# 203 groups of unread matmuls behind the last layer of a two-layer attention trunk

## The chip, the cores and the metric

The kernel runs on one core of one Trainium2 chip. The metric is the device time of one execution in microseconds. The profile is one execution with the hardware profiler on; its span goes from the first to the last instruction.

## The reference

The input x has 256 positions of 2048 channels. Two layers follow each other. A layer multiplies x with one wide matrix, cuts the result into queries, keys, values and gates of two attention branches with twelve heads each, does the attention of both, multiplies the gated results up to 2048 channels, mixes them with sigmoid gates, multiplies once more and normalises:

```python
h = jnp.einsum('bsd,dc->bsc', x, w_in)
...
out_a = dilated_mixture(qa, ka, heads(va, N_HEADS_A)).reshape(B, S, WIDTH_A)
up_a = jnp.einsum('bsw,wd->bsd', out_a * jax.nn.silu(za), w_up_a)
...
out_b = forgetting_attention(heads(qb, N_HEADS_B), heads(kb, N_HEADS_B),
                             heads(vb, N_HEADS_B), log_f).reshape(B, S, WIDTH_B)
up_b = jnp.einsum('bsw,wd->bsd', out_b * jax.nn.silu(zb), w_up_b)
...
y = jnp.einsum('bsd,de->bse', g_a * up_a + g_b * up_b, w_out)
return layer_norm(DEEPNORM_ALPHA * x + y, ln_g, ln_b)
```

The change adds nothing to what is computed.

## The kernel before

The state is kept transposed: channels in the partitions, the 256 positions (`S`) in the columns. So that the float32r matmuls keep their precision, every operand is held as two float32r numbers, a high part and a low part (`split`: ACT copies the high part, DVE subtracts). x lies in eight tiles `xs`, each for two blocks of 128 channels; `x_at(k)` is the block k with its high 256 columns followed by its low 256, 512 words in a row. There are sixteen such blocks (`KT`).

Weights come over the SP queue as pieces (`Piece`): mostly eight blocks of 128 x 128 for one output tile of 128 channels. A piece is split into a buffer `w` of 2240 words a partition, six of which are used in rotation. The high part begins at word 48 (`W_OFF`), the low part `W_PART` = 1088 words behind it. For the values the weights are 256 (once 268) columns wide and begin at word 16 (`V_OFF`).

A unit is one output tile of 128 channels. Its matmuls (`stat_mm`) keep the weights stationary and move x; they are pairs:

```python
            if part == 1:
                nc.tensor.matmul(o, w[:, 1], a[:, 0], start=False, stop=last)
            elif halves == 2:
                nc.tensor.matmul(ps(), w[:, 0], a, start=first, stop=False)
```

The high weights (line 161) move all 512 columns, the low weights (line 159) only the 256 high ones. Within a piece all `part` 0 go first and then all `part` 1, so runs of eight 512-column matmuls stand before runs of eight 256-column ones; the units over the gated heads have pieces of six blocks. Only in the three units that open a layer does each pair stand by itself, 512 and 256 columns in turn. The value units (`v_mm`, lines 345 to 352) are turned: x is stationary, the weights move (line 350: high and low weights of 256 columns each, line 352: high weights alone), for two output tiles in turn. The very last unit (lines 163, 164, 159) takes 256 columns at a time.

All these outputs are PSUM tiles `mm`, four in rotation, which ACT and DVE read out (lines 170 and 172; for the last projection 467 to 469). At the start, and between the layers, `keep_warm` adds matmuls of a zero tile whose result is not read (line 136).

Behind the last unit stands the normalisation: `second` sums over the channels by one-column matmuls (line 510), `ln_stats` forms mean and scale and spreads them over the partitions by matmuls again (line 523), and `ln_apply` normalises on DVE, ACT and GpSimd and stores the eight tiles over the SP queue (line 579).

The program is written unit by unit; a scheduler then orders each engine's instructions by their dependencies, so later work can be put between earlier work that waits. Each engine executes its own list in order.

Of the kernel before, what the change touches and what calls it, by code (L numbers as in the profile page):

```python
# [10 lines left out]
F32 = mybir.dt.float32  # L11
F32R = mybir.dt.float32r
# [6 lines left out]
S = 256  # L19
# [4 lines left out]
KT = D // 128  # L24
# [10 lines left out]
W_PART = (SLOT + 63) // 64 * 64  # L35
# [5 lines left out]
def trunk(ctx: ExitStack, tc: tile.TileContext, xt, w_st, w_v, w_vf, w_up, w_o,  # L41
          b_f, b_g, ln_g, ln_b, rope_c, bias_a, mask_c, ident_c, yt):
    nc = tc.nc
# [4 lines left out]
    wp = ctx.enter_context(tc.tile_pool(name="wp", bufs=1))  # L48
# [4 lines left out]
    pmm = ctx.enter_context(tc.tile_pool(name="pmm", bufs=4, space=PSUM))  # L53
# [554 lines left out]
    while n < len(units):  # L608
        k = 3 if n in interleaved else 1
# [55 lines left out]
    stats()  # L665
    for j2 in range(KT // 2):
        apply(j2)


def _tables():  # L670
# [78 lines left out]
```

## Time and profile before

| | us |
|---|---|
| median of two runs | 1984.47 (1984.30 to 1984.65) |
| profiled execution | 1984.45 |
| its span | 1982.7 |
| TensorE busy in the span | 1961.7 |
| VectorE (DVE) busy | 1269.7 |
| ScalarE (ACT) busy | 985.7 |
| GpSimd busy | 76.5 |
| mean granted TensorE clock | 0.994 |

The profiled execution is 1.75 us longer than its span: what lies ahead of the first and behind the last instruction. A busy engine is one with an instruction under way; matmuls overlap, so the number of matmuls times their mean duration is more than the busy time, and what one costs is read from the distance between two starts. In a timeline, a row merges instructions of one line that follow each other: its first number is the start of the first.

### The profile page before, as it was taken

The page shows a single profiled execution, that of the slowest core. Times are in us where ns is not written, and L with a number is a line of the kernel's source. Part 1 is how long each engine was busy: PE and PEld are TensorE (multiplying, and loading weights), DVE is VectorE, ACT ScalarE, POOL GpSimd, SP SyncE. Part 2 cuts the span into 40 slices and gives each one's busy share as a digit, 9 for nine tenths or more (in the row PEclk, how much of TensorE's full clock was granted, in tenths as well). Part 3 has the DMA queues.
Part 4 walks back from the last instruction along what each step waited for, and adds up shares of the span by engine and source line. Part 5 has one row for each costly group of instructions (what it writes and reads, how often), then busy time and mean ns, then how long its engine had stood idle before and what let it go on. Part 6 is the DMA issues. An engine that isn't in the chain of part 4 may idle for free.

```text
span 1982.7 us, 29718 instructions
## 1 busy us (share of the span) xinstructions
PE 1961.7 (99%) x11449; PEld 1730.0 (87%) x11449; DVE 1269.7 (64%) x1896; ACT 985.7 (50%) x1555; POOL 76.5 (4%) x69
## 2 busy tenths in 40 slices
PE   9999999999999999999999999999999999999997
PEld 7888888889888888888888888888898888888886
DVE  7666665556555556668777666655555555556686
ACT  5444444454444445554455444445454444545544
POOL 0000000001000000001200000000010000000022
PEclk9999999999999999999999999999999999999998
DMA  8655555666556655665555555566666655556651
GB/s 300 199 177 178 179 165 171 193 194 211 185 184 180 182 165 177 185 206 194 159 171 179 171 181 176 165 183 183 205 201 186 187 177 180 170 173 190 210 183 63
DMA packets 107766, 362.74 MB, mean 183 GB/s; under 512 B 12368, under 2 KB 15592, under 8 KB 107624
## 3 DMA queue, kind: packets, MB, share of 16 engines
q1 hardware_dynamic: 106600, 357.68, 58.2%
q0 software_dynamic: 1024, 3.17, 0.7%
q8 instruction: 89, 1.46, 0.3%
q14 instruction: 53, 0.43, 0.1%
HBM read 358.68 MB, written 2.12 MB: 182 GB/s over the span
## 4 chain that ended last, share of the span: by engine, by line
PE 98%; DVE 1%; ACT 0%; DMA 0%; issue 0%
PE mm L161 53%; PE mm L159 27%; PE mm L350 8%; PE mm L352 4%; PE ps_s L255 1%; PE po L284 1%; PE pt L275 1%; PE po L285 1%; PE ps_s L254 1%; DMA raw<-xt 0%; PE mm L348 0%; PE mm L345 0%; PE mm L346 0%; ACT gated L573 0%; PE mm L163 0%; PE mm L164 0%
## 5 line engine op out<-in xcount | busy, mean ns | idle before, releaser
L68 DVE TENSOR_TENSOR w<-raw,w 128x1024 fp32r<-128x1024 f32 (+3 forms) x713 | 840.3, 1183 | 448.4 <-ACT w L67 447.1
L67 ACT ACTIVATE w<-raw 128x1024 fp32r<-128x1024 f32 (+3 forms) x713 | 716.7, 1008 | 457.3 <-issue 221.8
L161 PE MATMUL mm<-x,w 128*128 128x512 f32 x3328 | 855.9, 396 | 7.5 <-DVE x L560 4.8
L161 PEld LDWEIGHTS mm<-x,w 128*128 128x128 f32 x3328 | 599.1, 188 | 116.9 <-issue 5.1
L159 PEld LDWEIGHTS mm<-x,w 128*128 128x128 f32 x3328 | 453.9, 188 | 34.2 <-DVE w L68 0.3
L159 PE MATMUL mm<-x,w 128*128 128x256 f32 x3328 | 469.6, 279 | 0.0
L170 ACT ACTIVATE c<-mm 128x256 f32<-128x256 f32 x320 | 120.4, 384 | 458.7 <-PE mm L159 425.0
L172 DVE TENSOR_TENSOR p<-mm,c 128x256 f32<-128x256 f32 x252 | 106.7, 424 | 185.9 <-ACT c L170 185.4
L161 PE MATMUL mm<-gated,w 128*128 128x512 f32 x768 | 196.5, 391 | 0.0
L350 PE MATMUL mm<-w,x 128*128 128x512 f32 x704 | 176.7, 393 | 0.0
L161 PEld LDWEIGHTS mm<-gated,w 128*128 128x128 f32 x768 | 135.2, 188 | 21.2
L350 PEld LDWEIGHTS mm<-w,x 128*128 128x128 f32 x704 | 126.1, 188 | 22.6
L161 PE MATMUL mm<-merged,w 128*128 128x512 f32 x480 | 120.1, 392 | 0.0
L159 PEld LDWEIGHTS mm<-gated,w 128*128 128x128 f32 x768 | 108.3, 188 | 10.4
L159 PE MATMUL mm<-gated,w 128*128 128x256 f32 x768 | 111.2, 279 | 0.0
L352 PEld LDWEIGHTS mm<-w,x 128*128 128x128 f32 x704 | 94.7, 188 | 7.4
L161 PEld LDWEIGHTS mm<-merged,w 128*128 128x128 f32 x480 | 85.9, 188 | 15.5 <-DVE merged L68 0.5
L352 PE MATMUL mm<-w,x 128*128 128x256 f32 x704 | 96.5, 279 | 0.0
L159 PEld LDWEIGHTS mm<-merged,w 128*128 128x128 f32 x512 | 68.2, 188 | 4.7
L159 PE MATMUL mm<-merged,w 128*128 128x256 f32 x512 | 70.1, 279 | 0.0
L444 POOL TENSOR_TENSOR u<-x 128x512 f32<-128x512 f32 x16 | 31.7, 1982 | 603.8 <-DVE merged L68 484.2
L264 ACT ACTIVATE z<-z,s 128x128 f32<-128x128 f32 x96 | 42.3, 444 | 0.0
(129 smaller groups left out, 918.0 us busy)
## 6 DMA issues: line engine op xcount, KB each, us to landing
raw<-w_st SPq DMA_DIRECT2D x410, 512.0 KB, 3.7
raw<-w_up SPq DMA_DIRECT2D x128, 384.0 KB, 3.2
raw<-w_v SPq DMA_DIRECT2D x88, 512.0 KB, 4.3
raw<-w_o SPq DMA_DIRECT2D x64, 512.0 KB, 3.7
raw<-w_vf SPq DMA_DIRECT2D x8, 536.0 KB, 3.7
nb<-cum POOLq DMA_DIRECT2D x12, 256.0 KB, 4.5
raw<-w_st SPq DMA_DIRECT2D x9, 256.0 KB, 5.6
yt<-gated SPq DMA_DIRECT2D x8, 256.0 KB, 2.1
```

Source lines behind the costliest of these rows:

```text
L67: nc.scalar.activation(hi, src, AF.Copy)
L68: nc.vector.tensor_tensor(lo, src, hi.bitcast(F32), op=ALU.subtract)
L159: nc.tensor.matmul(o, w[:, 1], a[:, 0], start=False, stop=last)
L161: nc.tensor.matmul(ps(), w[:, 0], a, start=first, stop=False)
L170: nc.scalar.activation(c, ps[:, S:], AF.Copy, scale=scale)
L172: nc.vector.tensor_tensor(dst, ps[:, :S], c, op=ALU.add)
L254: nc.tensor.matmul(ps[:, 0], q[:, :128], k[:, :128], start=True, stop=True)
L255: nc.tensor.matmul(ps[:, 1:3].rearrange("p a b -> p (a b)"), q[:, 128:], k, start=True, stop=True)
L264: nc.scalar.activation(z[:, sl], z[:, sl], AF.Exp, scale=-1.0, bias=s4[:, c:c + 1], accum_out=s4[:, 2 + c:3 + c])
L350: nc.tensor.matmul(o, xh, w, start=first, stop=False)
L352: nc.tensor.matmul(o[:, :NV], xl, w[:, 0], start=False, stop=last)
L444: nc.gpsimd.tensor_tensor(u, x[:, :, 0], x[:, :, 1], op=ALU.add)
```

## The change

A function `timing` is called behind the last layer. It takes two of the `w` buffers, fills them with zeros by two memsets on DVE, and issues matmuls of these weights with the x that the last layer was given. The results go into `mm` tiles and are not read.

`pairs(hi, lo, cut)` is one group of the first kind: sixteen pairs as in `stat_mm`, in runs of the lengths in `cut` (first the 512-column matmuls of the run, then its 256-column ones), the high weights beginning at word `hi` and the low ones at `W_PART + lo`. There are 3 groups of (8, 8), then for each run length of 1, 2, 4, 8 and 16 one group at each of the sixteen combinations of 0, 16, 32 and 48 for `hi` and `lo`, then eight uneven cuts three times each at four combinations. `turned(o, run)` is a group of the second kind, as in the value units, with two output tiles and the weights beginning at word `o`: three run lengths, four places, twice each. That makes 3 + 80 + 96 + 24 = 203 groups.

```diff
--- before.py
+++ after.py
@@ -665,6 +665,63 @@
     stats()
     for j2 in range(KT // 2):
         apply(j2)
+    timing(nc, wp, pmm, x_at)
+
+
+def timing(nc, wp, pmm, x_at):
+
+    ts = []
+    for _ in range(2):
+        t = wp.tile([128, 2 * W_PART + 64], F32R, name="w", tag="w", bufs=6)
+        nc.vector.memset(t.bitcast(F32), 0.0)
+        ts.append(t)
+
+    def pairs(hi, lo, cut):
+
+        p = pmm.tile([128, 2 * S], F32, name="mm", tag="mm")
+        k1 = 0
+        for run in cut:
+            k0, k1 = k1, k1 + run
+            for part in range(2):
+                for k in range(k0, k1):
+                    t = ts[k // 8]
+                    o = (lo + W_PART if part else hi) + k % 8 * 128
+                    w, a = t[:, o:o + 128], x_at(k)
+                    if part:
+                        nc.tensor.matmul(p[:, :S], w, a[:, 0], start=False, stop=k == KT - 1, skip_group_check=True)
+                    else:
+                        nc.tensor.matmul(p, w, a, start=k == 0, stop=False, skip_group_check=True)
+
+    for _ in range(3):
+        pairs(0, 0, (8, 8))
+    for run in (1, 2, 4, 8, 16):
+        for hi in (0, 16, 32, 48):
+            for lo in (0, 16, 32, 48):
+                pairs(hi, lo, (run,) * (16 // run))
+    for hi, lo in ((48, 48), (0, 48), (48, 16), (0, 16)):
+        for cut in ((6, 2, 8), (9, 7), (6, 10), (3, 5, 8), (11, 5), (14, 2), (6, 6, 4), (3, 3, 3, 3, 4)):
+            for _ in range(3):
+                pairs(hi, lo, cut)
+
+    def turned(o, run):
+
+        ps = [pmm.tile([128, 2 * S], F32, name="mm", tag="mm") for _ in range(2)]
+        for k0 in range(0, KT, run):
+            for part in range(2):
+                for k in range(k0, k0 + run):
+                    w = ts[k // 8][:, o:o + 2 * W_PART].rearrange("p (a b) -> p a b", a=2)
+                    w = w[:, :, k % 4 * S:(k % 4 + 1) * S]
+                    for t in range(2):
+                        xh, xl = (x_at(k)[:, c, t * 128:(t + 1) * 128] for c in range(2))
+                        if part:
+                            nc.tensor.matmul(ps[t][:, :S], xl, w[:, 0], start=False, stop=k == KT - 1, skip_group_check=True)
+                        else:
+                            nc.tensor.matmul(ps[t], xh, w, start=k == 0, stop=False, skip_group_check=True)
+
+    for run in (1, 2, 4):
+        for o in (0, 16, 32, 48):
+            for _ in range(2):
+                turned(o, run)
 
 
 def _tables():
```

On TensorE the built program puts the first matmuls of the first group between the statistics of the last normalisation. `lns`, `gated` and `sq` are what is summed, `mu` and `rs` what is spread, `mm` a tile of the added group:

```order
+L693 MATMUL mm<-x_81,w 128x512 x2
+L693 MATMUL mm<-x_82,w 128x512
 L510 MATMUL pst<-ones,gated 128x1 x2
+L693 MATMUL mm<-x_82,w 128x512
+L693 MATMUL mm<-x_83,w 128x512
 L510 MATMUL pst<-ones,sq 128x1 x2
+L693 MATMUL mm<-x_83,w 128x512
+L693 MATMUL mm<-x_84,w 128x512
 L523 MATMUL pm<-ident,mu 128x128 x2
+L693 MATMUL mm<-x_84,w 128x512
+L691 MATMUL mm<-x_81,w 128x256
 L523 MATMUL pa<-ident,rs 128x128 x2
```

Before, the statistics stood there alone and were the end of TensorE's list; now eight of the 512-column matmuls and one of the 256-column ones stand between them, and all other added matmuls behind them.

On DVE the two memsets stand behind the split of the last piece and ahead of the sum of the third output tile from the end:

```order
 L469 TENSOR_TENSOR gated<-gated,c 128x256
 L68 TENSOR_TENSOR w<-raw,w 128x1024
+L676 MEMSET w 128x2240 x2
 L468 TENSOR_TENSOR gated<-gated,mm 128x256
 L469 TENSOR_TENSOR gated<-gated,c 128x256
```

The sums behind them keep their order. The lists of ACT, GpSimd and SP hold what they held.

## Rows read from the trace of the kernel before

**Rows 1.** The page: its head, part 1 (busy time), part 4 (chain).

```profile
span 1982.7 us, 29718 instructions
...
PE 1961.7 (99%) x11449; PEld 1730.0 (87%) x11449; DVE 1269.7 (64%) x1896; ACT 985.7 (50%) x1555; POOL 76.5 (4%) x69
...
PE 98%; DVE 1%; ACT 0%; DMA 0%; issue 0%
```

**Rows 2.** Timeline of TensorE, runs of eight: start, us, engine, line, operation, count.

```profile
1311.80 2.00 PE L161 MATMUL mm<-x,w 128*128 128x512 f32 x8
1313.64 1.07 PE L159 MATMUL mm<-x,w 128*128 128x256 f32 x8
1314.55 1.99 PE L161 MATMUL mm<-x,w 128*128 128x512 f32 x8
1316.37 1.11 PE L159 MATMUL mm<-x,w 128*128 128x256 f32 x8
1317.32 2.00 PE L161 MATMUL mm<-x,w 128*128 128x512 f32 x8
```

**Rows 3.** Timeline of TensorE, runs of six.

```profile
1305.56 1.54 PE L161 MATMUL mm<-gated,w 128*128 128x512 f32 x6
...
1307.64 0.62 PE L161 MATMUL mm<-gated,w 128*128 128x512 f32 x2
```

**Rows 4.** Timeline of TensorE where 512 and 256 columns alternate.

```profile
1003.25 0.39 PE L161 MATMUL mm<-x,w 128*128 128x512 f32 x1
...
1004.31 0.39 PE L161 MATMUL mm<-x,w 128*128 128x512 f32 x1
```

**Rows 5.** Timeline of TensorE, a turned unit from its start to the next unit.

```profile
617.61 2.03 PE L350 MATMUL mm<-w,x 128*128 128x512 f32 x8
...
628.73 1.53 PE L161 MATMUL mm<-x,w 128*128 128x512 f32 x6
```

**Rows 6.** Timeline of TensorE, the end of its work (idle before, releaser).

```profile
1965.99 1.07 PE L159 MATMUL mm<-merged,w 128*128 128x256 f32 x8
1966.90 0.95 PE L510 MATMUL pst<-ones,lns 128*128 128x1 f32 x8
1967.71 0.58 PE L510 MATMUL pst<-ones,gated 128*128 128x1 f32 x4
1968.15 0.58 PE L510 MATMUL pst<-ones,sq 128*128 128x1 f32 x4
...
1969.92 1.22 PE L523 MATMUL pa<-ident,rs 128*128 128x128 f32 x4 [0.21 <-DVE rs L540]
```

**Rows 7.** Timeline of TensorE, weights of 268 columns moving.

```profile
453.64 1.15 PE L348 MATMUL mm<-w,x 128*128 128x268 f32 x8
454.62 0.29 PE L345 MATMUL mm<-w,x 128*128 128x268 f32 x1
...
456.48 0.28 PE L346 MATMUL mm<-w,x 128*128 128x268 f32 x1
```

**Rows 8.** Stretches: window, us, PE busy, granted clock, DMA share, GB/s.

```profile
990.00:992.00 2.00, 0.00 (x0) 0.50 0.00 0
...
996.00:998.00 2.00, 1.27 (x7) 0.80 0.00 0
...
1970.00:1972.00 2.00, 1.14 (x4) 0.50 0.00 0
```

**Rows 9.** Timeline of TensorE at the granted clock of 0.50.

```profile
993.65 0.63 PE L161 MATMUL mm<-x,w 128*128 128x512 f32 x1
...
994.29 0.63 PE L161 MATMUL mm<-x,w 128*128 128x512 f32 x1
```

**Rows 10.** Groups of instructions: a memset; timeline: a sum of the tail.

```profile
L130 DVE MEMSET warm<- 128x512 f32 x1 | 0.5, 485 | 0.9 <-PEq L741 0.9
...
1962.13 0.42 DVE L468 TENSOR_TENSOR gated<-gated,mm 128x256 f32<-128x256 f32 x1 [2.70 <-ACT c L467]
```

**Rows 11.** Timeline of TensorE at the start.

```profile
1.46 3.78 PE L136 MATMUL pw<-warm 128*128 128x512 f32 x8 [1.46 <-DVE warm L130]
```

## Prediction

> **What bounds the kernel now.** I read the page first. TensorE is busy for 1961.7 of the 1982.7 us of the span, and the chain that ended last lies on it for 98% [rows 1]. Whatever is queued on TensorE behind the last layer therefore lengthens the time by its own length, unless it fills idle time there. So the two things to read are how far apart the matmuls of the present kernel start (their durations overlap, so only the distance of the starts counts), and what TensorE does after its last real matmul.
>
> For the first I read TensorE in order of time. A product of two operands in two parts needs a pair for each block of 128 rows: a matmul of 512 columns (high weights on both parts of x) and one of 256 (low weights on the high part). In runs of eight, 16 pairs take 1317.32 - 1311.80 = 5.52 us, 345 ns a pair: 1.84 and 1.82 us for eight of 512 columns (229 ns each), 0.91 and 0.95 us for eight of 256 (114 and 118 ns) [rows 2]. In runs of six, 6 pairs take 2.08 us, 346.7 ns a pair [rows 3]. Where 512 and 256 columns alternate, three pairs take 1.06 us, 353.3 ns a pair [rows 4]. With the sides exchanged (x stationary, 2 x 256 weight columns moving, two output tiles), 32 pairs take 11.12 us, 347.5 ns a pair [rows 5]. So the run length moves a pair by 2 to 3%, no more, and the short runs are the dear ones.
>
> For the second I read the tail. The last real matmul ends its issue at 1966.90 us. Behind it stand eight, four, four, four and four records of the statistics, which wait for DVE in between, and the last of them starts in the group at 1969.92 us and ends at 1971.14 [rows 6]. The remaining 11 us of the span are ACT, DVE and GpSimd work and the stores; TensorE has nothing to do in them.
>
> **The change part by part.** *The count.* 3 + 80 + 96 groups are of the first kind, with 16 pairs each: 2864 pairs. 24 are turned, with two output tiles and so 32 pairs each: 768 pairs. Together 203 groups, 3632 pairs, 7264 matmuls. The built program holds all of them.
>
> *Their time at places that the kernel uses now.* Runs of one: 16 groups, 256 pairs x 353.3 ns = 90.4 us. Runs of two: no row shows them; between runs of one (353.3) and of six (346.7) I take 349 ns, 256 pairs, 89.3 us. All others in the first kind (147 groups, 2352 pairs; runs of 4, 8, 16 and the uneven cuts, most of them of 3 to 11): between 345 and 347.5 ns, I take 346.5, so 815.0 us. Turned, 256 pairs for each run length: with run one two 512 stand before two 256, like a run of two, 349; then 346.5; then the 347.5 of rows 5; together 267.0 us. Sum 1261.7 us.
>
> *Their time at other places.* Every weight in rows 2 to 4 stands 48 words behind the start of its buffer, in rows 5 16 words. The change uses 0, 16, 32 and 48. Foreign to the kernel are 15 of 16 combinations in the 80 groups, three of four in the 96, three of four offsets in the 24: 1200 + 1152 + 576 = 2928 pairs. The nearest rows are those of the one weight of 268 columns: its blocks are 1072 bytes apart, so they start at four different places within 256 bytes. There eight matmuls in a row take 0.98 us, 122.5 ns each, and the fifteen gaps of the mixed stretch behind them 1.86 us, 124.0 ns each [rows 7]; 268/256 of 114 to 118 ns would be 119 to 123. So a place costs some 1.5 ns a matmul on the mean: 2928 x 3 ns = 8.8 us. From below: nothing, or a gain, if the places used now are not the best. A gain ends where all pairs run at the best eighths of rows 2, 228 + 114 = 342 ns: 3632 x 342 = 1242 us. From above: 10 ns for each matmul of a foreign pair, the whole distance from the best 114 ns of rows 2 to the 124.0 of rows 7 with the wider columns in it; 58.6 us, so 1320 us. I take 1270.5.
>
> *Where they begin.* The order puts eight of 512 and one of 256 columns between the statistics matmuls, so they run in TensorE's waits there. If they filled every wait, the statistics would cost just 24 records x 0.11 us (0.44 us for four between 1967.71 and 1968.15) behind 1966.90, 1969.5; if nothing were filled, 1971.1. I take 1970.2: the waits for DVE's answers behind the sums (0.21 us and the issue around it ahead of the last one [rows 6]) remain in part. From there the 1270.5 us follow without a gap: the groups rotate through four PSUM tiles that nobody else reads, and the wait that the first matmul of a group carries is for one two or three groups back. Only the last turned group waits for its direct predecessor, once, about the 0.28 us of a matmul.
>
> *The clock.* TensorE was granted 0.50 at 1970 to 1972 us, and between the layers, after a similar thinning out, from 990 to 996.8 us (0.80 in the slice 996 to 998) [rows 8]. There a pair takes 0.64 us [rows 9]. If the added matmuls start under that, they lose half of up to 6.8 us; if the nine between the statistics keep the clock up, nothing. I take 1.5 of 0 to 3.4 us.
>
> *The two buffers.* Two memsets of 2240 columns are put on DVE between the last split and the sum of the third unit from the end. 512 columns took 485 ns [rows 10], so each takes about 2.1 us by that. Each waits for the matmuls of the weights that had the buffer before. DVE is idle for 2.70 us ahead of the sum at 1962.13 [rows 10], behind the sum that they may delay, and that takes up at least one of them. Cost nothing; with no such gap it would be 4.2 us in the tail, behind which TensorE has other work now. The normalisation and the stores end at 1980 to 1983 as before and are hidden under the added matmuls: no longer the end.
>
> *The end.* The span ends a matmul's duration (0.28 us [rows 7]) and a closing barrier behind the last start. No row shows the barrier apart from the last store; I take 0.9 us for both, with 0.3 and 3 as bounds. The sum: 1970.2 + 1270.5 + 1.5 + 0.9 = 3243.1 us of span. The profiled execution was 1984.45 us with a span of 1982.7, 1.75 us around it, and the median of the two runs 1984.47, the same. So **3245 us**.
>
> **The rivals.** *The columns alone.* The surplus of 16 ns over the bare columns (0.64 us a pair at half the clock is 320 ns at the full one [rows 9]) could come from DVE, ACT and the DMAs, which write and read the same memory all the time and are quiet in the added stretch. Then 3632 x 320 = 1162 us, and the time is 3137. Against it: at 1965.99, with the last weights long there and DVE nearly idle, eight of 256 columns still take 0.91 us [rows 6]. Chance 0.04. The Trainium skill, "TensorE: Matmul & The Clock Gate", section "Back-to-back issue gap", gives N/2.4 + 2.5 ns for an isolated matmul at the full clock; that is 325 ns a pair, 1180 us in all and an estimate of 3155 for the time. The trace speaks against it: 345 ns [rows 2].
>
> *Places that are dear.* If at some place the load of the next weights could no longer run under the moving columns, a matmul would pay a load more: four records of one column each take 0.44 us [rows 6], 110 ns each, nearly all of it load. A pair would then be 320 + 220 = 540 ns instead of 347. On a quarter of the foreign pairs that is 732 x 193 ns = 141 us, the time 3386; on half of them 3530. It decides from about 300 such pairs on, where it leaves my range. For it: no row has the weights and x at such places. Against it: the four starts of rows 7. Chance 0.09.
>
> *Not there at all.* Nobody reads what these matmuls write, and a stage behind the built program could drop them. Then the time is the 1984.5 of before, not slower; a change within 2%, about what a measurement of this kernel can tell from no change, needs fewer than some 110 pairs left. Against it: the warming matmuls of the first lines write a tile that nobody reads either, and they have records [rows 11]. Chance 0.01.
>
> *Half the clock throughout*, 640 ns a pair: 2324 us and a time of 4298. All dense slices of the page stand at the full clock. Chance 0.01.
>
> **How the numbers follow.** My forecast has 0.85: 3245, between the sum with 1242 us (3214 to 3217) and with 1320 (3295). The range reaches from 3215 to 3300; the cases outside it hold about 0.15 and a little of my own case's tails. Slower by over 2% is everything but the dropped matmuls: 0.985; within 2%: 0.012; faster 0.003.
>
> **What would show it.** In the profile after, pairs of lines 693 and 691 should start 353 ns apart in runs of one and 5.5 us for 16 in runs of eight, turned groups 11.1 us; nothing but TensorE after about 1985 us; the granted clock 1.00 from some us behind the statistics. Groups of the same cut that differ by several per cent between places would prove my 1.5 ns too small (or, if they are shorter than the native ones, of the wrong sign). A gap between groups would prove the rotation of the PSUM tiles wrong.

## The result, and the profile after

The changed kernel takes 3236.13 us (two runs, 3235.97 to 3236.29) against 1984.47 before: a ratio of 1.631 (1.629 to 1.634). The forecast was 3245, 9 us or 0.3% above it, with a range of 3215 to 3300.

The page of the changed kernel, in the parts of [rows 1]:

```profile
span 3234.5 us, 44248 instructions
...
PE 3224.0 (100%) x18713; PEld 2837.3 (88%) x18713; DVE 1272.5 (39%) x1898; ACT 986.2 (30%) x1555; POOL 76.7 (2%) x69
...
PE 99%; DVE 0%; DMA 0%; ACT 0%; issue 0%; SPq 0%
```

All 7264 matmuls are there (18713 - 11449), and what the other engines do has hardly changed. The timeline of TensorE where [rows 6] stood, and at the end:

```profile
1966.56 0.95 PE L510 MATMUL pst<-ones,lns 128*128 128x1 f32 x8
1967.37 0.94 PE L693 MATMUL mm<-x,w 128*128 128x512 f32 x3
...
1970.76 0.68 PE L523 MATMUL pa<-ident,rs 128*128 128x128 f32 x4
1971.20 1.08 PE L691 MATMUL mm<-x,w 128*128 128x256 f32 x7
...
3232.49 1.07 PE L717 MATMUL mm<-w,x 128*128 128x256 f32 x8
```

There is no idle time between the statistics any more. The stretches of the same time show the clock at 1.00 where [rows 8] had 0.50:

```profile
1968.00:1972.00 4.00, 4.00 (x31) 1.00 0.01 4
1972.00:1976.00 4.00, 4.00 (x24) 1.00 0.19 68
```

The timeline of TensorE in three groups, each from its first matmul to that of the next group. (48,0) stands for high weights from word 48 and low ones from word 0; (48,48) are the places that the kernel uses. The groups are (48,0) in runs of one, (48,48) in runs of one (compare [rows 4]) and (48,48) in runs of eight ([rows 2]):

```profile
2053.10 0.39 PE L693 MATMUL mm<-x,w 128*128 128x512 f32 x1
...
2058.54 0.39 PE L693 MATMUL mm<-x,w 128*128 128x512 f32 x1
...
2069.64 0.40 PE L693 MATMUL mm<-x,w 128*128 128x512 f32 x1
...
2075.29 0.62 PE L693 MATMUL mm<-x,w 128*128 128x512 f32 x2
...
2338.16 1.99 PE L693 MATMUL mm<-x,w 128*128 128x512 f32 x8
2339.99 1.10 PE L691 MATMUL mm<-x,w 128*128 128x256 f32 x8
2340.94 2.00 PE L693 MATMUL mm<-x,w 128*128 128x512 f32 x8
2342.78 1.10 PE L691 MATMUL mm<-x,w 128*128 128x256 f32 x8
2343.72 3.80 PE L693 MATMUL mm<-x,w 128*128 128x512 f32 x16
```

That is 5.44, 5.65 and 5.56 us for 16 pairs. At the old places the added groups run nearly as the kernel's own do, with every other engine quiet: 353.4 ns a pair in runs of one against 353.3 [rows 4], 347.2 in runs of eight against 345 [rows 2]. But runs of one are not dear at every place: (48,0) and (16,0) give the fastest groups of all, 340 and 341 ns a pair, and the sixteen groups in runs of one span 340 to 353 ns, with (0,0) and (16,16) as dear as (48,48).

| groups | pairs | forecast, us | measured, us | measured, ns a pair |
|---|---|---|---|---|
| the first three | 48 | 16.6 | 16.8 | 349 |
| runs of 1 | 256 | 91.1 | 89.2 | 348.5 |
| runs of 2 | 256 | 90.1 | 89.5 | 349.5 |
| runs of 4, 8, 16 | 768 | 268.3 | 268.2 | 349.2 |
| uneven cuts | 1536 | 535.7 | 533.1 | 347.1 |
| turned | 768 | 268.7 | 267.4 | 348.1 |
| sum | 3632 | 1270.5 | 1264.1 | 348.0 |

(The forecast's 3 ns a foreign pair is put to its groups. The first group, with the statistics in it, is counted with the time of the two groups like it.)

### The profile page after: what moved, and what is told of

It is laid out like the page before. It is cut to its first block, busy times and chain, and to the rows that moved or that the text cites. A ratio compares the mean times of both kernels' runs of the same rounds, so it can differ in the third digit from the quotient of the medians.

```text
span 3234.5 us, 44248 instructions
## 1 busy us (share of the span) xinstructions
PE 3224.0 (100%) x18713; PEld 2837.3 (88%) x18713; DVE 1272.5 (39%) x1898; ACT 986.2 (30%) x1555; POOL 76.7 (2%) x69
## 4 chain that ended last, share of the span: by engine, by line
PE 99%; DVE 0%; DMA 0%; ACT 0%; issue 0%; SPq 0%
PE mm L161 32%; PE mm L693 20%; PE mm L159 17%; PE mm L691 10%; PE mm L719 5%; PE mm L350 5%; PE mm L717 3%; PE mm L352 3%; PE ps_s L255 1%; PE po L284 1%; PE pt L275 0%; PE po L285 0%; PE ps_s L254 0%; DMA raw<-xt 0%; PE mm L348 0%; PE mm L345 0%
## 5 line engine op out<-in xcount | busy, mean ns | idle before, releaser
L161 PE MATMUL mm<-x,w 128*128 128x512 f32 x3328 | 855.7, 396 | 8.1 <-DVE x L560 4.8
L693 PE MATMUL mm<-x,w 128*128 128x512 f32 x2864 | 775.0, 393 | 0.0
L161 PEld LDWEIGHTS mm<-x,w 128*128 128x128 f32 x3328 | 599.3, 189 | 117.2 <-issue 5.1
L693 PEld LDWEIGHTS mm<-x,w 128*128 128x128 f32 x2864 | 502.1, 188 | 78.8
L159 PEld LDWEIGHTS mm<-x,w 128*128 128x128 f32 x3328 | 454.0, 188 | 33.9 <-DVE w L68 0.2
L159 PE MATMUL mm<-x,w 128*128 128x256 f32 x3328 | 469.5, 279 | 0.0
L691 PEld LDWEIGHTS mm<-x,w 128*128 128x128 f32 x2864 | 426.0, 188 | 43.6
L691 PE MATMUL mm<-x,w 128*128 128x256 f32 x2864 | 460.1, 280 | 0.0
L719 PE MATMUL mm<-w,x 128*128 128x512 f32 x768 | 214.1, 394 | 0.0
L350 PE MATMUL mm<-w,x 128*128 128x512 f32 x704 | 176.6, 393 | 0.0
L350 PEld LDWEIGHTS mm<-w,x 128*128 128x128 f32 x704 | 126.1, 188 | 22.6
L719 PEld LDWEIGHTS mm<-w,x 128*128 128x128 f32 x768 | 128.3, 188 | 14.0
L717 PEld LDWEIGHTS mm<-w,x 128*128 128x128 f32 x768 | 121.6, 188 | 19.4
L717 PE MATMUL mm<-w,x 128*128 128x256 f32 x768 | 125.9, 279 | 0.0
```

Of the source, the lines that this page charges most:

```text
L350: nc.tensor.matmul(o, xh, w, start=first, stop=False)
L691: nc.tensor.matmul(p[:, :S], w, a[:, 0], start=False, stop=k == KT - 1, skip_group_check=True)
L693: nc.tensor.matmul(p, w, a, start=k == 0, stop=False, skip_group_check=True)
L717: nc.tensor.matmul(ps[t][:, :S], xl, w[:, 0], start=False, stop=k == KT - 1, skip_group_check=True)
L719: nc.tensor.matmul(ps[t], xh, w, start=k == 0, stop=False, skip_group_check=True)
```

## The experiments

The sum came out; what was open was why a place and a run length matter. The theory: the distance between the starts of the weights and of the moving operand sets the time of a pair. The rivals: the order of what ran before, the numbers, or the work beside it. In the first six, `timing` is replaced, edited or called elsewhere; the other work is as in the changed kernel. Each of the six was executed once, and its readings are distances between starts within one execution.

**Ten groups of each of seven kinds**

```diff
+    for hi, lo, run in ((48, 0, 1), (16, 0, 1), (48, 48, 1), (48, 48, 8), (48, 16, 8), (0, 16, 16), (48, 0, 8)):
+        for _ in range(10):
+            pairs(hi, lo, (run,) * (16 // run))
```

> The added groups are replaced by ten each of seven kinds (high place, low place, run length). Place theory (where the weights start sets the time of a group, every time): (48,0) in runs of 1 stays at 5.44 us ten times over, (16,0) in runs of 1 at 5.46, (48,48) in runs of 1 at 5.65, (48,48) in runs of 8 at 5.51 to 5.56, (48,16) in runs of 8 at 5.50, (0,16) in runs of 16 at 5.54, (48,0) in runs of 8 at 5.59. History theory (a group's time hangs on what ran just before it, and the single measurements were chance): the ten of a kind drift or scatter by over 1%, and the seven means lie within 1% of 5.54.

2359.84 us. The ten groups of a kind agree within 10 ns from the second on: 5.440 us, 5.440, 5.648 to 5.657, 5.513, 5.493, 5.540 and 5.573. Only the first after a change of kind differs, by up to 56 ns. A scatter by chance falls; but (48,48) in runs of eight is 5.513 here and was 5.56 in the changed kernel, so a kind can have more than one value.

**The moving operand at word 0 or 16**

```diff
+    def moved(d):
+        return lambda k: ts[2][:, d + k % 4 * 512:d + k % 4 * 512 + 512].rearrange("p (a b) -> p a b", a=2)
```

> The moving operand is a zero tile that begins at word 0 or at word 16, in place of x. Relative theory (the distance between the weights' and the moving operand's start decides, in steps within 64 words): in runs of 1 the group of 5.44 us is (48,0) with the moving operand at 0 and (0,16) with it at 16, and the whole table of sixteen moves along by 16 words; 5.46 moves from (16,0) to (32,16). Absolute theory (the weights' own place decides): (48,0) takes 5.44 us at both. If neither, all groups of the second half differ by under 0.5%.

Runs of one, second group of two, us (the moving operand at 0, then at 16):

| at 0 | us | at 16 | us |
|---|---|---|---|
| (16,0) | 5.440 | (32,16) | 5.440 |
| (16,16) | 5.654 | (32,32) | 5.653 |
| (32,0) | 5.631 | (48,16) | 5.631 |
| (32,32) | 5.621 | (48,48) | 5.621 |
| (48,0) | 5.440 | (48,0) | 5.547 |
| (48,0) | 5.440 | (0,16) | 5.600 |

The start of the second group and of the group behind it, for (16,0) at 0, (32,16) at 16, (48,0) at 0 and (48,0) at 16:

```profile
2019.36 0.39 PE L693 MATMUL mm<-w 128*128 128x512 f32 x1
...
2024.80 0.39 PE L693 MATMUL mm<-w 128*128 128x512 f32 x1
...
2432.59 0.39 PE L693 MATMUL mm<-w 128*128 128x512 f32 x1
...
2438.03 0.39 PE L693 MATMUL mm<-w 128*128 128x512 f32 x1
...
2108.71 0.39 PE L693 MATMUL mm<-w 128*128 128x512 f32 x1
...
2114.15 0.39 PE L693 MATMUL mm<-w 128*128 128x512 f32 x1
...
2466.08 0.39 PE L693 MATMUL mm<-w 128*128 128x512 f32 x1
...
2471.63 0.40 PE L693 MATMUL mm<-w 128*128 128x512 f32 x1
```

Of the nine combinations that move by 16 words without passing a multiple of 64, eight agree within 1 ns; the ninth, (0,0), the first in line, does not (5.650 and 5.547). With the weights left where they are, 14 of 16 change by 22 ns or more, so the absolute theory falls. Of the seven that pass a multiple of 64, four agree within 6 ns and three do not, among them (48,0): these have a second value. In the runs of sixteen of the same experiment six of the nine agree within 2 ns and three differ by some 20 to 50 ns, and of the seven that pass a multiple of 64 three agree and four differ by 20 to 71. The distance explains most of the table, not all of it.

**One kind of matmul alone**

```diff
+    for cols in (2 * S, S):
+        for o in range(0, 68, 4):
```

> 32 matmuls of one kind in a row, weights at every fourth word from 0 to 64, first 512 columns, then 256. Place theory: 512 columns start every 226.7 ns at word 0, 233.5 at 16, 233 at 32, 229 at 48, and word 64 repeats word 0; 256 columns 119.8, 113.4 or 117.8, 120.2, 117.8; the words between lie between. Rival (the differences come only from the change between the two kinds): within one kind all places agree to 0.5 ns.

Mean distances from the thirteenth matmul on. 512 columns: 226.7 ns at words 0, 4, 60 and 64; 230 to 234 at all others, also at 48 (233.4), where runs of eight had 229. 256 columns: 113.3 at 16, 120.0 at 0 and 64, 116.7 to 120.1 elsewhere. So the place matters within one kind, word 64 repeats word 0, and good places differ for the two kinds. Each place was run once, in rising order, so what ran ahead is not varied here.

**Numbers in place of zeros**: eight copies of x into the weights.

```diff
+        for i in range(4):
+            nc.vector.tensor_copy(t[:, i * 512:(i + 1) * 512].rearrange("p (a b) -> p a b", a=2), x_at(i).bitcast(F32))
```

> As the changed kernel, but the weights are x's numbers in place of zeros. Both theories of place and history: 3236 us plus up to 3 for the eight copies ahead, groups as before within 0.02 us. Rival (zeros run faster than numbers, by a lower clock under load): the added stretch is longer by several per cent, or the granted clock below 1.00 in it.

3240.19 us. Every group has the time that it had with zeros, within 1 ns, but the first (6 ns); the granted clock is 1.00. The 4 us are not the copies: the layers ahead ran longer in this execution. The second layer's first matmuls over `merged`, in the changed kernel (1877.55) and here (1881.46), and the first DVE instructions of `timing` here:

```profile
1877.55 1.31 PE L161 MATMUL mm<-merged,w 128*128 128x512 f32 x5
...
1881.46 0.85 PE L161 MATMUL mm<-merged,w 128*128 128x512 f32 x3
...
1957.68 1.93 DVE L676 MEMSET w<- 128x2240 f32 x1 [0.42 <-issue]
1959.64 0.76 DVE L678 CAST w<-x 128x512 fp32r<-128x512 f32 x2
```

All 3.9 us are there 76 us before the first memset, and the added matmuls begin 3.9 us later too. The numbers do not matter here.

**Everything behind the normalisation**

```diff
+    with tc.issue_after(ins.ins):
+        timing(nc, wp, pmm, x_at)
```

> The changed kernel with the two memsets and all added matmuls behind the last DVE instruction of the normalisation, so nothing stands between the statistics and TensorE is idle in between. By my sum: the added stretch begins at about 1983 us instead of 1967 and takes its 1264 us whole, so the time is 3236 + 14 = 3250 us if the clock stands at full speed at its start, and up to 3.4 more if it begins at half: 3250 to 3254, with the granted clock 0.50 in the first microseconds. Rival (the early start hid nothing, the order of the end is what counts): 3236.

3252.75 us. The timeline of TensorE where the added stretch begins, and its stretches (columns as in [rows 8]):

```profile
1983.84 3.75 PE L695 MATMUL mm<-x,w 128*128 128x512 f32 x8 [10.96 <-DVE w L678]
1987.39 1.35 PE L693 MATMUL mm<-x,w 128*128 128x256 f32 x8
1988.58 2.00 PE L695 MATMUL mm<-x,w 128*128 128x512 f32 x8
```

```profile
1984.00:1988.00 4.00, 4.00 (x12) 0.51 0.01 4
1988.00:1992.00 4.00, 4.00 (x26) 1.00 0.00 0
```

After 11 us of idle time the first piece takes 4.74 us instead of 2.8 (1988.58 to 1991.37 for the next one in this trace): about 2 us lost to the half clock, inside my 0 to 3.4. Of the 16.6 us above the changed kernel 2.6 are again the layers ahead, whose statistics begin at 1969.16 instead of 1966.56. The other 14 are 12 us of waits that nothing fills (the 11 and the gaps between the statistics) and the 2 of the clock, which the early start of the changed kernel saved. The rival, 3236, falls.

**Other matmuls between the groups**

```diff
+    def other(cols):
...
+        for n in cols:
+            nc.tensor.matmul(p[:, :n], ts[0][:, :128].bitcast(F32), ts[1][:, :n].bitcast(F32), start=True, stop=True)
...
+                for cols in ((128, 256, 128, 256), (128, 128, 128), (256, 256, 128, 128, 128, 128, 128), (256, 128)):
+                    other(cols)
+                    pairs(hi, lo, (run,) * (16 // run))
```

> Groups of all sixteen combinations of places, in runs of 1 and of 8, four of each, and ahead of each group some plain float32 matmuls like those of the attention, in four forms. Two-rhythm theory (a place allows two or more steady rhythms, and what runs ahead of a group picks one): (48,0) in runs of 1 takes 5.44 us after some forms and 5.61 after others, and a group keeps its rhythm from its third pair to its end; (48,48) in runs of 8 takes 5.51 or 5.57. Rival (in the working part DVE, ACT and the DMAs beside it make the slower pairs): here, where all these are quiet, every group of (48,0) takes 5.44 and every one of (48,48) 5.51, but for its first pair.

2835.74 us. Group (48,0) in runs of one, behind the first form and behind the second:

```profile
2295.71 0.40 PE L693 MATMUL mm<-x,w 128*128 128x512 f32 x1
2295.94 0.28 PE L691 MATMUL mm<-x,w 128*128 128x256 f32 x1
2296.06 0.40 PE L693 MATMUL mm<-x,w 128*128 128x512 f32 x1
...
2300.61 0.83 PE L700 MATMUL mm<-w 128*128 128x128 f32 x6
...
2302.66 0.39 PE L693 MATMUL mm<-x,w 128*128 128x512 f32 x1
2302.88 0.28 PE L691 MATMUL mm<-x,w 128*128 128x256 f32 x1
2303.00 0.39 PE L693 MATMUL mm<-x,w 128*128 128x512 f32 x1
```

350 ns a pair (233 + 117) from the second pair to the last behind the first form, against 340 (227 + 113) from the third pair on behind the second. Behind the third and fourth form it is 340 as well, from the fifth and the third pair on. The same weights, x and order, with all else quiet: two rhythms, picked by what ran ahead. (48,48) in runs of eight has two values too: from its ninth 512-column matmul to its last matmul, 2.627 us behind the first and third form and 2.667 behind the others. (16,0), 5.440 in the first experiment, stays near 350 behind all four forms.

**Four versions of the kernel without added matmuls.** In pieces of 128 columns the pairs alternate, or the low part gets another place, or both:

```diff
             o = W_OFF if self.w == 128 else V_OFF
-            self.t = t[:, o:o + 2 * W_PART].rearrange("p (a b) -> p a b", a=2)
+            d = 1040 if self.w == 128 else W_PART
+            self.t = t[:, o:o + 2 * d].rearrange("p (a b) -> p a b", a=2)
...
-            for part in range(2):
-                for i in range(len(g[0].kts)):
-                    g[0].run(i, part)
+            n = len(g[0].kts)
+            steps = [(i, part) for part in range(2) for i in range(n)]
+            if g[0].w == 128:
+                steps.sort()
+            for i, part in steps:
+                g[0].run(i, part)
```

> The kernel before, nothing added; in pieces of 128 columns the pairs alternate (512, 256, 512, 256) and the low part begins at a multiple of 64 words (place 0) instead of word 48. Place theory: the 4576 pairs of these units go from about 346 ns to 340.5, so 25 us less, 1959 us. Rival (in the working part the pace is set by DVE, ACT and the DMAs beside it): no change beyond 3 us.

> The kernel before with the alternation alone, places as they are (48,48). Place theory: 353.3 ns in place of 346 a pair, 33 us more, 2017 us. Rival (alternation is what helps): 1959 us here too. Rival (the work beside it sets the pace): no change beyond 3 us.

> The kernel before with the low part at place 0 alone, runs of eight as they are. Place theory: 349.2 ns a pair, about 15 us more, 1999 us. Rival (place 0 alone is what helps): 1959 us. Rival (the work beside it sets the pace): no change beyond 3 us.

> The kernel before with the low part at place 16, runs of eight as they are. Place theory: 343.8 ns a pair instead of 346, about 10 us less, 1974 us. Rival (the work beside it sets the pace): no change beyond 3 us.

(For place 16, d is 1056.) A fifth, with the high part at 16 and the low at 0:

> The kernel before, nothing added, alternating pairs, the high weights at place 16 and the low ones at place 0: the other combination at 340 ns a pair. Place theory with one rhythm: 1959 us, as was expected of (48,0), which gave 1968.7. Two-rhythm theory: between 1959 and 1984, by how many units fall into the slower rhythm after the attention's matmuls; over 1968.7 or under it is open.

The pair (the mean distances from its two kinds of matmul to the next start, added, those over 400 ns left out) is given for 330 to 430 us, gate and up units, and for 130 to 230 us, where the attention's matmuls stand between the units:

| version | us | ratio to before | pair, up units, ns | pair, attention, ns |
|---|---|---|---|---|
| before, (48,48), runs of 8 | 1983.5 | | 345.5 | 348.9 |
| alternating, (48,0) | 1968.7 | 0.9924 (0.9909 to 0.9939) | 340.0 | 346.6 |
| alternating, (48,48) | 2006.2 | 1.0112 (1.0095 to 1.0129) | 348.9 | 353.7 |
| (48,0), runs of 8 | 1997.9 | 1.0071 (1.0056 to 1.0086) | 348.7 | 351.0 |
| (48,16), runs of 8 | 1984.5 | 1.0005 (0.9995 to 1.0014) | 343.8 | 350.2 |
| alternating, (16,0) | 2001.7 | 1.0087 (1.0070 to 1.0105) | 350.0 | 352.7 |

(Before: the median beside the first four; beside the fifth it was 1984.1.) The signs of the first three are the theory's, and place 0 and alternation each harm alone and help together. Of the sizes only the third came out (14 us of 15): the others are 15 us in place of 25, 23 in place of 33, nothing in place of 10, and (16,0) lies outside all that was expected. In the up units (48,0) and (48,16) show exactly the 340.0 and 343.8 of the unread groups; what is missing there is lost between the attention's matmuls. Alternating (48,48) and (16,0) run at another value even in the up units, 348.9 and 350.0 in place of 353 and 340. For (48,0) the trace sorts it out: the 48 units behind score or value matmuls run at 340 to 342 ns, 46 of the 48 behind transposes at 350. These 46 x 16 pairs x 10 ns are 7 of the 10 us that are missing.

**Choosing the rhythm**, built on the alternating (48,0):

```diff
+            alone = lambda: flip(0)
+            alone.skew = True
...
-                    [lambda: flip(0)],
-                    [lambda: values(0), lambda: flip(1)],
+                    [alone],
+                    [lambda: flip(1), lambda: values(0)],
...
+                if g[0].first and any(hasattr(f, "skew") for f in jobs.get(n0, [])):
+                    steps[1:3] = steps[2:0:-1]
```

> The version with alternating pairs and the low weights at place 0, with two edits: the transposes of a pair's second head stand ahead of the value matmuls of its first head instead of behind them (24 units), and the unit behind the transposes of a first head begins with two matmuls of 512 columns before two of 256 (24 units). Two-rhythm theory (what ran last before a unit picks its rhythm): the first 24 units go from 350 ns a pair to 340, as all units behind value matmuls do, 3.8 us less than 1968.7, about 1965; the second 24 go to 340 as well if the two 512 shift the phase, 3.8 us more, about 1961, or stay at 350. Rival (the attention's DVE and ACT work at that time, not the last matmuls, makes the 350): all 48 units stay at 350 and the time at 1968.7.

1965.46 us, a ratio of 0.990 (0.988 to 0.992): 18 us under the kernel before and the fastest here, though the interval overlaps that of the alternating version. What each edit did is read from the trace. A unit behind transposes, in the alternating version and in this one:

```profile
203.52 0.40 PE L162 MATMUL mm<-x,w 128*128 128x512 f32 x1
203.75 0.28 PE L160 MATMUL mm<-x,w 128*128 128x256 f32 x1
203.87 0.40 PE L162 MATMUL mm<-x,w 128*128 128x512 f32 x1
```

```profile
202.52 0.70 PE L162 MATMUL mm<-x,w 128*128 128x512 f32 x2
203.06 0.40 PE L160 MATMUL mm<-x,w 128*128 128x256 f32 x2
203.30 0.39 PE L162 MATMUL mm<-x,w 128*128 128x512 f32 x1
203.52 0.28 PE L160 MATMUL mm<-x,w 128*128 128x256 f32 x1
203.64 0.39 PE L162 MATMUL mm<-x,w 128*128 128x512 f32 x1
```

The 24 units that begin with two of 512 columns all went to 340 or 341 ns. The 24 behind the exchanged transposes and value matmuls all stayed at 350, though value matmuls now ran last before them. So what ran last does not pick the rhythm by itself, and there my expectation was wrong; more of the sequence ahead counts. The work of DVE and ACT falls as the cause in the first 24, which have the same work beside them and another order of two matmuls.

## Why the prediction was right

- *Count and length.* The groups follow each other without a gap, as forecast, and take 1264.1 us instead of 1270.5. The 6.4 us are most of the miss of 9; the rest is 0.9 in the start and 1.5 in the clock, less 0.2 at the end. The 6.4 us sit in the uneven cuts (2.6), the runs of one (1.9), the turned groups (1.3) and the runs of two (0.6).
- *Run length.* This step failed in kind: "the short runs are the dear ones". [Rows 4] showed one place, which is as dear here (353.4 ns). Over all places the run lengths lie between 348.5 and 349.7 ns, and runs of one are the cheapest. Runs of two, put at 349 at the kernel's own places without a row, were 346.1 there.
- *Places.* Taken apart, both terms were a little high. At the kernel's own places the sum would be 1257.8 us in place of 1261.7. A foreign place costs 2.2 ns a pair on the mean in place of 3, so 6.3 us in place of 8.8. But that mean joins unlike numbers: -5.2 ns in runs of one, 3.6 in runs of two, 2.8 in runs of 4 to 16, 2.6 in the uneven cuts and 3.0 in the turned groups. In runs of one the sign is the other one, which the prediction had named as a proof against its 1.5 ns, and groups of one cut differ by up to 4%. That the mean came so near is partly luck: the 122.5 and 124.0 ns of [rows 7] scarcely leave the 119 to 123 that the width alone gives there. The bounds held: single groups lie between 340 and 354 ns a pair, the turned ones between 345 and 351, where 342 and 363 were the bounds of the mean. That some places are better than the native one, which I kept as the lower bound, holds: 340 under the 342 of the best eighths of [rows 2].
- *Where they begin.* From the end of 3233.4 us, 1264.1 back is 1969.3, against 1970.2: the waits were filled but for 0.1 us (24 records of 0.111 behind 1966.56 are 1969.2), and the part ahead ended 0.3 us earlier (1966.56). That end varies from one execution to the next: it came at 1969.16 and at 1970.47 in two of those above.
- *Clock.* No loss in place of 1.5: the nine matmuls between the statistics left no idle time, and the granted clock stayed at 1.00. With nothing between them, in the version behind the normalisation, it was 2.
- *Memsets.* 1.93 us each instead of 2.1; the delay is made up before the next sum, which is no later than in [rows 10]. DVE in the changed kernel:

```profile
1953.77 1.93 DVE L676 MEMSET w<- 128x2240 f32 x1 [0.42 <-issue]
1956.30 1.93 DVE L676 MEMSET w<- 128x2240 f32 x1 [0.60 <-PE mm L159]
...
1961.79 0.42 DVE L468 TENSOR_TENSOR gated<-gated,mm 128x256 f32<-128x256 f32 x1 [0.90 <-ACT c L467]
```

- *End.* 1.1 us of span behind the end of the stream of matmuls instead of 0.9, and 1.8 around the span of the profiled execution (3236.29 - 3234.5) as before.
- *Rivals.* The surplus over the bare columns, 16 ns in the prediction, is 345 - 320 = 25 by its own rows; its 3137 follows from the 320 and stands. This rival falls: with everything else quiet a native group in runs of eight takes 5.51 to 5.56 us, as beside full traffic. Dear places, dropped matmuls and half the clock do not occur. The estimate of 3155 by the Trainium skill's formula ("TensorE: Matmul & The Clock Gate", "Back-to-back issue gap") misses by 23 ns a pair, after 20 in [rows 2]; no place here reaches its 325 ns.

Why a distance of some words costs up to 13 ns a pair, and what the two rhythms are in the machine, was not settled. The runs show that the time of a pair depends on the two operands' distance and on the sequence ahead; it did not change with the numbers, and both rhythms appear with the other engines quiet.

## What to carry to other kernels

Matmuls behind the end of a kernel that TensorE bounds cost their own length; a sum of distances between starts gave it to within 0.5%, with one step wrong in it. Where these distances vary by some ns in a trace, try where the operands begin and in which order the kinds alternate, both together: each alone made this kernel slower (0.7 and 1.1%), together 0.8% faster. Then time the kernel itself: (16,0), as fast as (48,0) in unread groups, made it 0.9% slower. One measurement of one place is one rhythm; repeat it behind the work that will stand ahead of it.

## What was not expected of the hardware

A stream of identical pairs at (48,0) settles in one of at least two rhythms, 340 or 350 ns, and keeps it for a whole unit; two matmuls exchanged at its start moved it from one to the other. And the good place is narrow: 256 columns take 113.3 ns with the weights from word 16, 117.7 from word 12 and 118.8 from word 20.
